# Hybrid Fourier and RG-LRU layer: the gate part of the adaLN product moved from GpSimd to narrow TensorE matmuls

## The chip, the cores and the metric

One core of a Trainium2 chip, one launch, all data in f32. The metric is the device time of a launch in microseconds, and of several launches the median.

## The reference

One layer of a diffusion backbone: a latent stream of 2048 positions by 1024 channels, with a context of 256 positions in front. A conditioning vector c gives shift, scale and gate through one product with w_ada (1024 by 3072). The modulated stream is projected into two branches with a gate path each: a 2-D Fourier transform (FNet) and a convolution with a bidirectional gated recurrence (RG-LRU, 4 heads). Both are gated, joined and projected out; the result is multiplied by `gate`, added to the stream and normalised.

```
def modulate(x, g, shift, scale):
    return rmsnorm(x, g) * (1.0 + scale) + shift
...
mod = jax.nn.silu(c) @ w_ada[l] + b_ada[l]
shift, scale, gate = jnp.split(mod[:, None, :], 3, axis=-1)
...
hx = modulate(x, norm_gain[l], shift, scale)
...
uf_x, gf_x, ul_x, gl_x = in_proj(hx, w_in[l])
...
r = jax.nn.sigmoid(block_diag(u, w_rg, b_rg).astype(jnp.float32))
i = jax.nn.sigmoid(block_diag(u, w_ig, b_ig).astype(jnp.float32))
log_a = -LRU_C * r * jax.nn.softplus(-lam.astype(jnp.float32))
a = jnp.exp(log_a)
bx = jnp.sqrt(-jnp.expm1(2.0 * log_a)) * (i * u.astype(jnp.float32))
...
y = jnp.concatenate([y_f * jax.nn.silu(g_f), y_l * jax.nn.silu(g_l)], axis=-1)
return y @ w_out
```

The change concerns only the columns of `mod` that become `gate` (the last 1024 of 3072), for the latent stream, and the order in which the second stage's work is written down.

## The kernel before

The program runs in stages on the one core. Stage 1 (list `S1`) does the modulation, the projections into the branches and the first transform; then comes the Fourier branch (list `STEPS`); stage 2 (list `S2`) does the projection into the gate path and the whole recurrence; stage 3 (list `S3`) does the output projection. Every list is a string of tokens. A token is one step of one helper, and PE, ACT and DVE take their instructions in exactly the order in which the tokens write them (manual_schedule, L718). The queues of SP and POOL are ordered by the framework's scheduler.

Nearly every product is done in three matmuls (mm3, L71 to L73): each f32 operand is split into a high part (cast on ACT) and a low part (subtraction on DVE).

The tokens of stage 2 that the text speaks of:

- `B0` to `B31` (p2_block): a block of the gate-path projection, 48 matmuls of 128x256 from `hg` and `wg` into a PSUM tile `pg`. `H` loads a piece of the modulated stream (L684), `Q` casts its high part on ACT (L689), `q` its low part on DVE (L694). `V` and `v` copy a finished `pg` out on ACT or DVE (L744), and a POOL queue stores it.
- `L`, `C`, `c` (L666 to L670, L785, L792): load a piece of a head, first tap of the convolution on ACT, three taps on DVE. `X` and `x` split the result `v` into `vh` (ACT, L798) and `vl` (DVE, L806) and the gate weights into their two parts (L802, L809).
- `g` (lru_gate): the recurrence's gate products from `vh`, `vl` and `gw`: `pl`, two stretches of 512 columns in a pool of its own (psl, 2 buffers), and for the first piece of a head also `pc`, 256 columns of context, in the pool ps2. Piece p has four of them, `gp.0` to `gp.3`. `S`, `T`, `E`, `R` on ACT and `s`, `I`, `N` on DVE (sigmoid, tanh, exp, root; products and scans) turn them into the recurrence.
- `G` (load_gate, L678): loads two of the eight pieces `gb` of w_ada's gate columns for one quarter q; two buffers. `A` (ada_gate) multiplies each piece with the silu of c (`sc_pad`) and sums it up, on GpSimd: L752 the product, L755 and L758 the sum of a piece's two halves, L759 the sum with `gsb`. `F` (ada_gate_fin) sums `gsb` over the partitions with a matmul of ones (L763, tile `go`) and adds it to `gate_bc` on DVE (L764). There are four quarters, and two `A` in each: 16 products and 28 sums.

The pool ps2 has four buffers of one bank, which `pg`, `pc` and `go` take in turn. In stage 1 the shift and scale columns of the same product are done by narrow matmuls on TensorE (ada_part, L131): 32 columns of `sc_pad` are the stationary operand, and four column groups of the array write four groups of 32 partitions of one PSUM tile.

The functions that the diff touches:

Of the kernel before, what the change touches and what calls it, by code (L numbers as in the profile page):

```python
# [9 lines left out]
F32 = mybir.dt.float32  # L10
# [42 lines left out]
def tile_layer(ctx, tc, xp, xnat, xt_in, ctxn, ctxt, w_ada, vec, bgate, fgain, w_in, w_g, w_four, w_gate, w_out,  # L53
               dct, d512, rmat, csts, out):
    nc = tc.nc
# [22 lines left out]
    sel, wsc = cst[:, 0:2], cst[:, 2:7]  # L78
    ones = const.tile([P, P], F32, name="ones")
# [9 lines left out]
    sc_pad = const.tile([P, KD, 32], F32, name="sc_pad")  # L89
# [24 lines left out]
    blks, raws, parts, pws = {}, {}, {}, {}  # L114
# [378 lines left out]
    p2 = p2s.enter_context(tc.tile_pool(name="p2", bufs=1, side="right", reuse_waits="tile"))  # L493
# [155 lines left out]
    X0 = CTX + GAP  # L649
# [75 lines left out]
    ps2 = pst.enter_context(tc.tile_pool(name="ps2", bufs=4, space=PSUM, reuse_waits="tile"))  # L725
# [21 lines left out]

    def ada_gate(q, h):
        for j in (2 * h, 2 * h + 1):
            blk = gbs.pop((q, j))  # L750
            cv = sc_pad[:, 2 * j:2 * j + 2, 0:1].to_broadcast([P, 2, 256])
            nc.gpsimd.tensor_tensor(out=blk, in0=blk, in1=cv, op=ALU.mult)  # L752
            if j == 0:
                acc = parts[q] = p2.tile([P, 256], F32, name=f"gsb{q}", tag="gsb", bufs=1)
                nc.gpsimd.tensor_tensor(out=acc, in0=blk[:, 0], in1=blk[:, 1], op=ALU.add)  # L755
            else:
                acc = parts[q]
                nc.gpsimd.tensor_tensor(out=blk[:, 0], in0=blk[:, 0], in1=blk[:, 1], op=ALU.add)  # L758
                nc.gpsimd.tensor_tensor(out=acc, in0=acc, in1=blk[:, 0], op=ALU.add)  # L759

    def ada_gate_fin(q):
        po = ps2.tile([P, 512], F32, name=f"go{q}", tag="pg")
        nc.tensor.matmul(po[:, 0:256], ones, parts.pop(q), start=True, stop=True)  # L763
        nc.vector.tensor_tensor(out=gate_bc[:, 256 * q:256 * q + 256], in0=gate_bc[:, 256 * q:256 * q + 256],  # L764
                                in1=po[:, 0:256], op=ALU.add)
# [92 lines left out]
    def lru_root(hd, pc):  # L858
        w, ts = WID[pc], st_[hd, pc][2]
        for d in range(2):  # L860
            nc.scalar.activation(out=ts[d][:, 0:w], in_=ts[d][:, 0:w], func=AF.Sqrt)
# [139 lines left out]
    def p3_lo(b, q, e):  # L1001
# [10 lines left out]
        "R": lambda p: lru_root(*pieces[p]), "I": lambda p, d: lru_input(*pieces[p], d), "N": lambda p, d: lru_scan(*pieces[p], d),  # L1012
        "A": ada_gate, "G": load_gate, "F": ada_gate_fin,
        "W": load_wo, "o": wo_gate, "O": wo_hi, "u": wo_tail,
        "Y": lambda i: (p3_first_load, p3_first_act, p3_first_prep)[i](ob[0]),
    }
    for x in S2:
        ops[x[0]](*(int(c) for c in x[1:].split(".")))
    xs, pos, s3 = {}, {}, {}
# [203 lines left out]
```

## Time and profile before

| | |
|---|---|
| Median of 3 runs | 677.46 us (676.71, 681.53, 677.46) |
| Span of the profiled execution, first to last instruction | 676.5 us |
| PE busy | 655.5 us, 97% of the span |
| DVE busy | 494.3 us, 73% |
| ACT busy | 403.2 us, 60% |
| POOL busy | 165.0 us, 24% |
| of which gate products and sums, L752, L755, L758, L759 | 23.1, 4.0, 15.7, 17.2 us |
| Stage 1 and Fourier branch | 0 to about 243 us |
| Stage 2 on PE | about 243 to 491.9 us |
| Stage 3 on PE | 492.0 to 676.5 us |

The profile is of one execution. The profiled execution has no device time of its own on record beside its span; the median of the three timed runs lies 1.0 us above that span. Busy shares are means over stages with different limits, so the rows further down are taken from the stage that the change touches. A PE matmul is pipelined: the step from one start to the next tells what it costs, and the duration in a row is longer. A plain f32 matmul shows as two instructions.

### The profile page before, as it was taken

To read this page: it belongs to the slowest core of one execution; us is meant where nothing else is said; L and a number is where in the kernel's file an instruction comes from. 1 tells how busy PE (TensorE), PEld (TensorE's weight loads), DVE (VectorE), ACT (ScalarE), POOL (GpSimd) and SP (SyncE) were. 2 spreads that over 40 slices of the span, in tenths; PEclk is the share of its full clock that TensorE was granted. 3 is DMA by queue.
4 is the path that set the end of the run, shared out by engine and by line. 5 is a ranking of instruction groups with operands and counts; after the bars stand their busy time and mean duration, and the time that the engine had idled before them with its cause. 6 is when DMAs were issued, how large, how long until landed. Compare 5 with 4: busy or idle time off the path is not lost.

```text
span 676.5 us, 10651 instructions
## 1 busy us (share of the span) xinstructions
PE 655.5 (97%) x4060; PEld 579.4 (86%) x4060; DVE 494.3 (73%) x767; ACT 403.2 (60%) x578; POOL 165.0 (24%) x214
## 2 busy tenths in 40 slices
PE   9999999999989989999996999999999999999996
PEld 8888888888978879899996999999988888888885
DVE  4767999877646697567999899997989455544523
ACT  5475777565624445577785877977753465543502
POOL 0000101031320276339756145131210000000000
PEclk8999999999988999999999899999999999999999
DMA  8996876548695884344443353432479566775211
GB/s 335 419 335 225 257 263 212 193 121 253 163 310 188 276 286 118 109 125 119 153 144 99 111 175 106 126 131 79 135 255 344 186 215 232 245 261 180 88 62 63
DMA packets 69898, 130.21 MB, mean 192 GB/s; under 512 B 7090, under 2 KB 39986, under 8 KB 69848
## 3 DMA queue, kind: packets, MB, share of 16 engines
q1 hardware_dynamic: 51080, 82.36, 37.0%
q0 software_dynamic: 12384, 39.00, 17.2%
q10 hardware_dynamic: 6384, 8.18, 3.7%
q8 instruction: 32, 0.52, 0.3%
q14 instruction: 18, 0.15, 0.1%
HBM read 91.24 MB, written 38.27 MB: 191 GB/s over the span
## 4 chain that ended last, share of the span: by engine, by line
PE 71%; DVE 13%; issue 5%; ACT 5%; DMA 4%; POOL 1%; DVEq 0%; SPq 0%; ACTq 0%; POOLq 0%
PE po L71 9%; PE po L72 9%; PE po L73 9%; PE pul L71 4%; PE pul L73 4%; PE pul L72 4%; PE pg L72 4%; PE pg L73 4%; PE pg L71 4%; DVE t L865 3%; PE ptt L71 2%; PE ptt L73 2%; PE ptt L72 2%; DVE v L792 2%; DVE t L872 1%
## 5 line engine op out<-in xcount | busy, mean ns | idle before, releaser
L71 PE MATMUL pg<-hg,wg 128*128 128x256 f32 x512 | 144.7, 283 | 1.9 <-DVE yf L646 1.9
L72 PE MATMUL pg<-hg,wg 128*128 128x256 f32 x512 | 144.3, 282 | 2.1 <-DVE hg L694 2.1
L73 PE MATMUL pg<-hg,wg 128*128 128x256 f32 x512 | 144.4, 282 | 0.3 <-DVE wg L545 0.3
L71 PE MATMUL po<-wo,y 128*128 128x512 f32 (+1 forms) x264 | 102.4, 388 | 0.0
L72 PE MATMUL po<-wo,y 128*128 128x512 f32 (+1 forms) x264 | 102.3, 387 | 0.0
L73 PE MATMUL po<-wo,y 128*128 128x512 f32 (+1 forms) x264 | 102.3, 387 | 0.0
L72 PEld LDWEIGHTS pg<-hg,wg 128*128 128x128 f32 x512 | 96.9, 189 | 3.5 <-DVE hg L694 2.5
L71 PEld LDWEIGHTS pg<-hg,wg 128*128 128x128 f32 x512 | 96.9, 189 | 3.3 <-ACT wg L544 2.3
L73 PEld LDWEIGHTS pg<-hg,wg 128*128 128x128 f32 x512 | 97.0, 189 | 0.5 <-DVE wg L545 0.5
L424 POOL DMA_DIRECT2D g_d<-gs x80 | 57.9, 725 | 96.7 <-DVE gs L744 53.0
L71 PEld LDWEIGHTS po<-wo,y 128*128 128x128 f32 x264 | 49.9, 189 | 11.0
L73 PEld LDWEIGHTS po<-wo,y 128*128 128x128 f32 x264 | 49.6, 188 | 11.2
L72 PEld LDWEIGHTS po<-wo,y 128*128 128x128 f32 x264 | 49.6, 188 | 10.7
L71 PE MATMUL pul<-hl,wu 128*128 128x512 f32 x124 | 49.9, 402 | 0.0
L1066 ACT ACTIVATE j<-xr 128x1024 bf16<-128x1024 f32 x15 | 15.9, 1058 | 55.5 <-DVE xr L1061 55.5
L73 PE MATMUL pul<-hl,wu 128*128 128x512 f32 x124 | 48.9, 395 | 0.0
L72 PE MATMUL pul<-hl,wu 128*128 128x512 f32 x124 | 48.8, 394 | 0.0
L1076 POOL DMA_DIRECT2D out_dram<-xr x15 | 8.0, 533 | 136.2 <-DVE xr L1075 136.2
L792 DVE SCALAR_TENSOR_TENSOR v<-up,vecs,v 128x1284 f32<-128x1284 f32 (+1 forms) x24 | 40.2, 1676 | 1.2 <-ACT v L785 0.6
L836 ACT ACTIVATE g<-pl,vecs 128x1024 f32<-128x1024 f32 x32 | 35.3, 1115 | 8.4 <-PE pl L73 8.4
L287 ACT ACTIVATE h<-xt,sh,gn 128x512 f32<-128x512 f32 x31 | 25.2, 813 | 19.4 <-DVE gn L149 10.4
L71 PE MATMUL ptt<-wf,eo 128*128 128x260 f32 (+1 forms) x128 | 36.5, 285 | 0.0
(298 smaller groups left out, 1569.8 us busy)
## 6 DMA issues: line engine op xcount, KB each, us to landing
xt<-in_xt_dram SPq DMA_DIRECT2D x16, 512.0 KB, 5.6
blk<-in_w_ada_dram SPq DMA_DIRECT2D x16, 512.0 KB, 8.1
hr<-h_d SPq DMA_DIRECT2D x32, 256.0 KB, 3.8
xr<-in_xnat_dram SPq DMA_DIRECT2D x16, 512.0 KB, 3.6
g<-g_d SPq DMA_DIRECT2D x15, 512.0 KB, 5.1
out_dram<-xr POOLq DMA_DIRECT2D x15, 512.0 KB, 2.9
dm<-in_dct_dram POOLq DMA_DIRECT2D x12, 514.0 KB, 6.7
x<-in_xp_dram SPq DMA_DIRECT2D x12, 512.0 KB, 5.6
```

The costliest lines, as they stand in the source:

```text
L71: nc.tensor.matmul(out_, lh, rh, start=first, stop=False, skip_group_check=skip)
L72: nc.tensor.matmul(out_, lh, rl, start=False, stop=False, skip_group_check=skip)
L73: nc.tensor.matmul(out_, ll, rh, start=False, stop=last, skip_group_check=skip)
L287: nc.scalar.activation(out=h[:, 0:n], in_=x, func=AF.Identity, scale=g, bias=b)
L424: queue.dma_start(dst[:, :, row:row + s1 - s0], s[:, :, P * i - off + s0:P * i - off + s1])
L792: nc.vector.scalar_tensor_tensor(out=v[:, 0:w], in0=up[:, j:j + w], scalar=cw[:, j:j + 1], in1=v[:, 0:w], op0=ALU.mult, op1=ALU.add)
L836: nc.scalar.activation(out=t[:, c0:c0 + cn], in_=pg[:, 0:cn], func=AF.Sigmoid, bias=vecs[:, q:q + 1])
L865: nc.vector.tensor_tensor_scan(sl(t), sl(a), sl(t), init, ALU.mult, ALU.add)
L872: nc.vector.tensor_tensor(out=t[:, 0:w], in0=t[:, 0:w], in1=iv[:, 0:w], op=ALU.mult)
L1066: nc.scalar.activation(out=junk, in_=xs[b][t], func=AF.Square, accum_out=s3[b, t][:, 0:1])
L1076: nc.gpsimd.dma_start(out[256 * b + P * t:256 * b + P * t + P], o)
```

## The change

The gate product of a quarter becomes eight narrow matmuls of `sc_pad` and `gb`, four in each `A`, into a PSUM tile `gpart` from the pool ps2; they are the same form as stage 1's. A new token `a` (ada_gate_copy) copies `gpart` to `gsb` on DVE, and the matmul in `F` takes a broadcast column of `sel` in place of ones. GpSimd does no arithmetic of it any more. The list `S2` is written in a new order; `S1`, `STEPS` and `S3` are as before.

```diff
@@ -39,7 +39,7 @@
-S2 = "H1.0 C0 c0 L1 X0 x0 Q1.0 H1.1 Q1.1 q1.1 q1.0 H1.2 B0 v0 ...
-    s0.2 A0.1 C2 X1 q1.3 x1 g0.3 S0.3 B7 Q2.1 Q2.0 c2 B4 T0 R0 ...
-    B8 H3.2 C3 Q3.0 V7 H3.3 g2.0 T1 s1.2 G2.0 q3.0 Q3.1 q3.1 c3 L4 E1 R1 v8 I1.1 S2.0 A1.1 N1.1 B9 ...
+S2 = "H1.1 H1.2 C0 H1.0 c0 Q1.1 X0 x0 Q1.0 H2.2 q1.1 q1.0 L1 B0 v0 ...
+    C2 X1 q1.3 g0.3 B7 A0.1 a0 Q2.0 Q2.1 S0.3 c2 x1 B4 T0 R0 ...
+    B8 A1.0 T1 G1.1 C3 Q3.0 V7 x2 H3.2 g2.0 s1.2 s1.1 R1 c3 q3.0 H4.1 Q3.1 q3.1 A1.1 E1 L4 v8 I1.0 I1.1 N1.1 B9 ...
 RB = 6
 SR = 72
 ZB = 7
@@ -746,21 +746,23 @@
         scatter(dst, gs, u, nc.gpsimd, (2 * hf, 2 * hf + 1), 256 * hf)
 
     def ada_gate(q, h):
+        if h == 0:
+            parts[q] = ps2.tile([P, 512], F32, name=f"gpart{q}", tag="pg")
         for j in (2 * h, 2 * h + 1):
             blk = gbs.pop((q, j))
-            cv = sc_pad[:, 2 * j:2 * j + 2, 0:1].to_broadcast([P, 2, 256])
-            nc.gpsimd.tensor_tensor(out=blk, in0=blk, in1=cv, op=ALU.mult)
-            if j == 0:
-                acc = parts[q] = p2.tile([P, 256], F32, name=f"gsb{q}", tag="gsb", bufs=1)
-                nc.gpsimd.tensor_tensor(out=acc, in0=blk[:, 0], in1=blk[:, 1], op=ALU.add)
-            else:
-                acc = parts[q]
-                nc.gpsimd.tensor_tensor(out=blk[:, 0], in0=blk[:, 0], in1=blk[:, 1], op=ALU.add)
-                nc.gpsimd.tensor_tensor(out=acc, in0=acc, in1=blk[:, 0], op=ALU.add)
+            for i in range(2):
+                g = (2 * j + i) % 4
+                nc.tensor.matmul(parts[q][32 * g:32 * g + 32, 0:256], sc_pad[:, 2 * j + i, :], blk[:, i, :],
+                                 start=h == 0, stop=h == 1, tile_position=(0, 32 * g))
+
+    def ada_gate_copy(q):
+        part = parts.pop(q)
+        parts[q] = p2.tile([P, 256], F32, name=f"gsb{q}", tag="gsb", bufs=1)
+        nc.vector.tensor_copy(parts[q], part[:, 0:256])
 
     def ada_gate_fin(q):
         po = ps2.tile([P, 512], F32, name=f"go{q}", tag="pg")
-        nc.tensor.matmul(po[:, 0:256], ones, parts.pop(q), start=True, stop=True)
+        nc.tensor.matmul(po[:, 0:256], sel[:, 0:1].to_broadcast([P, P]), parts.pop(q), start=True, stop=True)
         nc.vector.tensor_tensor(out=gate_bc[:, 256 * q:256 * q + 256], in0=gate_bc[:, 256 * q:256 * q + 256],
                                 in1=po[:, 0:256], op=ALU.add)
 
@@ -1010,7 +1012,7 @@
         "g": lambda p, i: lru_gate(*pieces[p], MS[i]), "S": lambda p, i: lru_sig(*pieces[p], MS[i]),
         "s": lambda p, i: lru_gated(*pieces[p], MS[i]), "T": lambda p: lru_tanh(*pieces[p]), "E": lambda p: lru_exp(*pieces[p]),
         "R": lambda p: lru_root(*pieces[p]), "I": lambda p, d: lru_input(*pieces[p], d), "N": lambda p, d: lru_scan(*pieces[p], d),
-        "A": ada_gate, "G": load_gate, "F": ada_gate_fin,
+        "A": ada_gate, "a": ada_gate_copy, "G": load_gate, "F": ada_gate_fin,
         "W": load_wo, "o": wo_gate, "O": wo_hi, "u": wo_tail,
         "Y": lambda i: (p3_first_load, p3_first_act, p3_first_prep)[i](ob[0]),
     }
```

Three places in the new order follow. Names carry the number of their tile, which differs between the two programs; lines from L764 on stand two lines further down in the changed kernel.

PE from the end of block `B8` (`pg_0_0`) to the start of `B9` (`pg_0_1`), before; `pc` and `pl` are the product `g2.0`:

```order
L73 MATMUL pg_0_0_3478<-hg_0_3_3420,wg_0_2759 128x256
L71 MATMUL pc_0_3543<-vh_0_3469,gw_3472 128x256
L72 MATMUL pc_0_3543<-vl_0_3470,gw_3472 128x256
L73 MATMUL pc_0_3543<-vh_0_3469,gw_3472 128x256
L71 MATMUL pl_0_0_260_3547<-vh_0_3469,gw_3472 128x512
L72 MATMUL pl_0_0_260_3547<-vl_0_3470,gw_3472 128x512
L73 MATMUL pl_0_0_260_3547<-vh_0_3469,gw_3472 128x512
L71 MATMUL pl_0_0_260_3547<-vh_0_3469,gw_3472 128x512
L72 MATMUL pl_0_0_260_3547<-vl_0_3470,gw_3472 128x512
L73 MATMUL pl_0_0_260_3547<-vh_0_3469,gw_3472 128x512
L71 MATMUL pg_0_1_3599<-hg_0_0_3219,wg_0_2379 128x256
```

The place from behind `B8` on now, where `gpart` is the narrow product of quarter 1 (each row of x2 is two matmuls):

```order
L755 MATMUL gpart_3515<-gb_0_3284,sc_pad 32x256 x2
L755 MATMUL gpart_3515<-gb_1_3286,sc_pad 32x256 x2
L71 MATMUL pc_0_3544<-vh_0_3459,gw_3462 128x256
L72 MATMUL pc_0_3544<-vl_0_3460,gw_3462 128x256
L73 MATMUL pc_0_3544<-vh_0_3459,gw_3462 128x256
L71 MATMUL pl_0_0_260_3548<-vh_0_3459,gw_3462 128x512
L72 MATMUL pl_0_0_260_3548<-vl_0_3460,gw_3462 128x512
L73 MATMUL pl_0_0_260_3548<-vh_0_3459,gw_3462 128x512
L71 MATMUL pl_0_0_260_3548<-vh_0_3459,gw_3462 128x512
L72 MATMUL pl_0_0_260_3548<-vl_0_3460,gw_3462 128x512
L73 MATMUL pl_0_0_260_3548<-vh_0_3459,gw_3462 128x512
L755 MATMUL gpart_3515<-gb_2_3524,sc_pad 32x256 x2
```

The two halves of quarter 1 now stand on PE around `g2.0`, nine matmuls apart (`A1.0` with `gb_0` and `gb_1`, then `A1.1`, which begins with `gb_2`); before, PE had nothing of them.

SP's queue at the loads of the second half of quarter 1 (`gb_2`, `gb_3`) and the first of quarter 2 (`gb_0`, `gb_1`), before:

```order
L684 DMA hr_1_3_3539<-h_d 128x2x256
L678 DMA gb_2_3429<-in_w_ada_dram 128x512
L659 DMA gwr_3570<-in_w_gate_dram 128x512
L678 DMA gb_3_3431<-in_w_ada_dram 128x512
L684 DMA hr_0_1_3650<-h_d 128x2x256
L684 DMA hr_0_0_3824<-h_d 128x2x256
L678 DMA gb_0_3559<-in_w_ada_dram 128x512
```

And now:

```order
L684 DMA hr_1_2_3540<-h_d 128x2x256
L659 DMA gwr_3574<-in_w_gate_dram 128x512
L678 DMA gb_2_3524<-in_w_ada_dram 128x512
L678 DMA gb_3_3526<-in_w_ada_dram 128x512
L678 DMA gb_0_3642<-in_w_ada_dram 128x512
L678 DMA gb_1_3644<-in_w_ada_dram 128x512
L666 DMA up_0_3576<-ul_d 128x256
```

The four loads stand in a row behind the load of the gate weights `gwr`. The two buffers of `gb` are still there, so a load waits for the reader of the piece before it: a POOL product before, a PE matmul now.

DVE at the split of the first head's second piece (`vl_1`, token `x1`), before; `v_0` are the taps `c2` of the next head, L840 is `s`:

```order
L840 TENSOR_TENSOR g_0_0_3036<-g_0_0_3036,v_0_2810 128x1284
L840 TENSOR_TENSOR g_0_0_3104<-g_0_0_3104,v_0_2810 128x1284
L694 TENSOR_TENSOR hg_1_3_2969<-hr_1_3_2890,hg_1_3_2969 128x512
L806 TENSOR_TENSOR vl_1_3149<-v_1_2894,vh_1_3148 128x1024
L819 MEMSET g_0_0_3153 128x4
L792 SCALAR_TENSOR_TENSOR v_0_3146<-up_0_2958,vecs,v_0_3146 128x1284 x3
L694 TENSOR_TENSOR hg_0_1_3217<-hr_0_1_3128,hg_0_1_3217 128x512
```

And now; `gsb` is the new copy `a0`:

```order
L842 TENSOR_TENSOR g_0_0_3106<-g_0_0_3106,v_0_2812 128x1284
L694 TENSOR_TENSOR hg_1_3_2967<-hr_1_3_2946,hg_1_3_2967 128x512
L821 MEMSET g_0_0_3141 128x4
L761 COPY gsb_3207<-gpart_3018 128x256
L794 SCALAR_TENSOR_TENSOR v_0_3135<-up_0_2956,vecs,v_0_3135 128x1284 x3
L808 TENSOR_TENSOR vl_1_3138<-v_1_2892,vh_1_3137 128x1024
L694 TENSOR_TENSOR hg_0_1_3211<-hr_0_1_3104,hg_0_1_3211 128x512
```

The split stands behind the copy and behind the three taps, where it stood ahead of the taps.

## Rows read from the trace of the kernel before

**Rows 1.** What PE waited for between 236 and 500 us: total, times, longest.

```profile
PE pc L72 <- DVE vl L806: 5.5, 1, 5.5
PE pg L72 <- DVE hg L694: 2.1, 2, 1.3
PE pg L71 <- DVE yf L646: 1.9, 1, 1.9
PE pc L71 <- ACT gs L744: 0.6, 1, 0.6
PE pl L72 <- DVE vl L806: 0.4, 1, 0.4
PE pg L73 <- DVE wg L545: 0.3, 1, 0.3
```

**Rows 2.** PE's timeline at the longest wait: start, duration, instruction, idle before it.

```profile
371.74 0.58 PE L72 MATMUL pc<-vl,gw 128*128 128x256 f32 x1 [5.46 <-DVE vl L806]
```

**Rows 3.** Busy time by stretch (columns named in the first line).

```profile
core 0: us, PE busy (x) PEld busy (x) DVE busy (x) ACT busy (x) POOL busy (x), PEclk, DMA share, GB/s
317.00:371.00 54.00, 48.45 (x367) 46.13 (x365) 53.20 (x44) 40.07 (x44) 37.08 (x34) 1.00 0.43 133
371.50:375.00 3.50, 3.24 (x8) 2.47 (x9) 3.46 (x5) 3.47 (x4) 0.53 (x1) 0.50 0.70 213
375.00:380.00 5.00, 5.00 (x33) 4.90 (x32) 2.58 (x7) 4.97 (x6) 1.44 (x2) 0.73 0.45 127
380.00:440.00 60.00, 60.00 (x454) 57.48 (x453) 57.60 (x54) 47.28 (x52) 21.54 (x24) 1.00 0.41 125
```

**Rows 4.** Groups on DVE between 317 and 371 us: count, busy us, mean ns.

```profile
L792 DVE SCALAR_TENSOR_TENSOR v<-up,vecs,v 128x1284 f32<-128x1284 f32 x3 | 6.2, 2056 | 0.1
...
L792 DVE SCALAR_TENSOR_TENSOR v<-up,vecs,v 128x1024 f32<-128x1024 f32 x3 | 5.0, 1680 | 0.1
L872 DVE TENSOR_TENSOR t<-t,g 128x1284 f32<-128x1284 f32 x2 | 4.1, 2071 | 0.1
...
L840 DVE TENSOR_TENSOR g<-g,v 128x1024 f32<-128x1024 f32 x2 | 3.3, 1640 | 0.0
```

**Rows 5.** Groups of two of these kinds on DVE from 456 us on.

```profile
L872 DVE TENSOR_TENSOR t<-t,g 128x1284 f32<-128x1284 f32 x2 | 3.0, 1496 | 0.1
...
L840 DVE TENSOR_TENSOR g<-g,v 128x1024 f32<-128x1024 f32 x2 | 2.4, 1208 | 0.0
```

**Rows 6.** DVE's timeline: single instructions, two of them beside an idle POOL.

```profile
282.94 1.55 DVE L792 SCALAR_TENSOR_TENSOR v<-up,vecs,v 128x1284 f32<-128x1284 f32 x1
...
370.20 1.48 DVE L806 TENSOR_TENSOR vl<-v,vh 128x1284 fp32r<-128x1284 f32 x1
...
372.81 1.28 DVE L792 SCALAR_TENSOR_TENSOR v<-up,vecs,v 128x1024 f32<-128x1024 f32 x1
```

**Rows 7.** DVE's timeline ahead of the first block of stage 2.

```profile
239.09 2.18 DVE L694 TENSOR_TENSOR hg<-hr,hg 128x512 fp32r<-128x512 f32 x2
241.19 2.55 DVE L545 TENSOR_TENSOR wg<-wgr,wg 128x512 fp32r<-128x512 f32 x2
...
250.88 0.68 DVE L545 TENSOR_TENSOR wg<-wgr,wg 128x512 fp32r<-128x512 f32 x1
```

**Rows 8.** PE's timeline in stage 1: narrow matmuls (L131) and what follows them.

```profile
47.48 1.07 PE L131 MATMUL part<-blk,sc_pad 128*32 128x256 f32 x16
48.48 0.50 PE L71 MATMUL pul<-hl,wu 128*128 128x512 f32 x1
48.81 0.39 PE L72 MATMUL pul<-hl,wu 128*128 128x512 f32 x1
49.04 0.39 PE L73 MATMUL pul<-hl,wu 128*128 128x512 f32 x1
```

**Rows 9.** Tile `gb`: from its load's issue to landing, us, min/median/max.

```profile
DMA to landing us min/median/max: 2.4/3.0/7.3
```

**Rows 10.** Line L137, the copy of stage 1's narrow product: duration ns min/median/max.

```profile
L137 DVE COPY psb<-part x8: 414/424/427, 13.3 to 62.5; 128x256 f32<-128x256 f32 x8
```

More of the change, by code (lines that the diff above doesn't have):

```diff
@@ new lines @@
+S2 = "H1.1 H1.2 C0 H1.0 c0 Q1.1 X0 x0 Q1.0 H2.2 q1.1 q1.0 L1 B0 v0 C1 c1 B1 H1.3 G0.1 Q1.2 L2 V1 Q1.3 B2 A0.0 g0.0 g0.1 S0.1 B3 H2.0 S0.0 q1.2 H2.1 g0.2 V3 s0.1 v2 S0.2 s0.2 C2 X1 q1.3 g0.3 B7 A0.1 a0 Q2.0 Q2.1 S0.3 c2 x1 B4 T0 R0 q2.1 v4 F0 G1.0 E0 B5 L3 I0.1 Q2.2 H2.3 q2.2 g1.0 g1.1 S1.0 q2.0 B6 v5 Q2.3 q2.3 N0.1 S1.1 H3.1 I0.0 g1.3 N0.0 H3.3 H3.0 g1.2 V6 X2 S1.2 S1.3 B8 A1.0 T1 G1.1 C3 Q3.0 V7 x2 H3.2 g2.0 s1.2 s1.1 R1 c3 q3.0 H4.1 Q3.1 q3.1 A1.1 E1 L4 v8 I1.0 I1.1 N1.1 B9 G2.0 g2.1 S2.1 S2.0 a1 B10 s2.1 g2.2 Q3.2 Q3.3 S2.2 V10 V9 q3.2 s2.2 H4.0 B11 F1 Q4.1 V11 C4 g2.3 X3 q3.3 x3 S2.3 Q4.0 c4 L5 H4.2 T2 H4.3 N1.0 E2 q4.1 R2 q4.0 B12 A2.0 v12 g3.0 B13 G2.1 I2.1 N2.1 I2.0 g3.1 S3.1 Q4.2 S3.0 s3.1 B14 q4.2 Q4.3 g3.2 N2.0 V14 S3.2 g3.3 s3.2 X4 H5.1 v13 x4 S3.3 q4.3 C5 c5 L6 T3 H5.0 A2.1 G3.0 H5.2 E3 B15 H5.3 a2 g4.0 R3 S4.0 v15 I3.1 Q5.0 B16 F2 N3.1 B17 Q5.2 Q5.1 q5.0 V16 g4.1 Q5.3 S4.1 g4.2 g4.3 q5.2 S4.2 s4.2 V17 A3.0 B18 S4.3 B19 C6 I3.0 H6.3 s4.1 X5 q5.1 H6.0 N3.0 q5.3 G3.1 v18 x5 c6 L7 v19 T4 R4 H6.1 E4 g5.0 I4.1 S5.0 Q6.0 g5.1 A3.1 I4.0 N4.1 S5.1 a3 s5.1 B20 Q6.1 H6.2 V20 N4.0 B21 F3 g5.2 v21 g5.3 Q6.2 S5.2 s5.2 Q6.3 q6.2 X6 x6 q6.0 q6.1 S5.3 C7 B22 c7 T5 R5 q6.3 E5 v22 I5.0 g6.0 B23 g6.1 S6.0 I5.1 B24 N5.1 g6.2 v24 V23 H7.0 N5.0 S6.1 S6.2 H7.1 g6.3 s6.1 s6.2 Q7.0 H7.2 X7 Q7.2 Q7.1 B25 H7.3 x7 S6.3 q7.0 q7.2 q7.1 T6 Q7.3 R6 W0 g7.0 v25 W3 q7.3 E6 S7.0 W1 B26 I6.1 o1 N6.1 g7.1 S7.1 s7.1 B27 V26 V27 Y0 Y1 o0 W2 W4 g7.2 Y2 O1 o2 W6 W7 O2 O0 o3 u2 W5 I6.0 u1 S7.2 o4 O3 g7.3 s7.2 S7.3 T7 u0 W10 W9 E7 O4 u3 N6.0 o5 o6 O6 O5 o7 u6 B28 u5 B29 W8 v29 O7 B30 v28 B31 u4 W11 u7 R7 V30 V31".split()
```

1 line of the change is left out of this document (removed).

## Prediction

> **What bounds the kernel now.** I read the busy shares first: PE works 97% of the span, so the time is PE's own work plus the few places where PE stands still. Next come PE's waits, to find those places. All that count lie in stage 2 [rows 1]: one wait of 5.5 us for `vl`, two for `hg` (2.1 together), 1.9 for `yf`, and three small ones, 10.8 us in all (5.5 + 2.1 + 1.9 + 0.6 + 0.4 + 0.3). Except for the 0.6, which waits for ACT to empty a bank, they wait for DVE. The long one is the first product with `vl` of piece 4 (token `g4.0`) at 371.74 [rows 2].
>
> Then the stretches [rows 3]. Before that wait DVE is busy 53.2 of 54 us: it is the engine that is late. After it the granted clock of PE is 0.50 until 375 and 0.73 until 380, then 1.00 again. That is the lower of its levels (1.2 of 2.4 GHz), after PE had stood still for 5.46 us. From 371.74 to 375 at half speed loses 1.6 us and 5 us at 0.73 lose 1.35: about 3 us more for the same stall.
>
> Last, why DVE is late. In the same stretch POOL is busy 37.1 us [rows 3], and DVE's instructions take longer than elsewhere: the taps 2056 and 1680 ns against 1.55 and 1.28 us, L872 2071 against 1496, L840 1640 against 1208 [rows 4 to 6]. Those four groups alone are 1.5 + 1.2 + 1.15 + 0.86 = 4.7 us over their usual durations. They are 10 of the 44 instructions; I estimate the whole stretch at 7.7 us by working the other groups in the same way.
>
> **GpSimd's arithmetic goes.** 16 products and 28 sums, 60 us on POOL by the table. POOL is not the bound, so this gives nothing by itself. What it gives is DVE's delay back. At the first block of stage 2 four instructions of two kinds take 2.18 and 2.55 us for two, where one alone of the second kind takes 0.68 [rows 7]: 2.55 - 1.36 = 1.2 us on one pair, and there are two pairs of each kind ahead of the second block, some 4 us. So the waits for `yf` (1.9) and `wg` (0.3) should go.
>
> The Trainium skill, "SBUF — State Buffer", section "Terms", says that GpSimd and DVE take one pair of ports under an exclusive lock and that the loser blocks for the whole instruction. By that rule taken alone, DVE could lose most of POOL's 37 us in the stretch; the rows show a fifth of that, so the sum goes by the rows.
>
> **The long wait.** DVE ends `vl` at 370.20 + 1.48 = 371.7 [rows 6]. Without the stretch it is 364.0 to 367.0 (less 7.7 or 4.7), plus two new copies `a0` and `a1` ahead of it, at 0.42 each by stage 1's copy [rows 10]: 364.8 to 367.8. PE came to the place at 371.74 - 5.46 = 366.3. Now it comes earlier by the waits ahead of it (1.9 + 0.3 + 0.6 + 2.1 = 4.9) and later by six narrow sets (3.6, below) and one new wait (1.5, below): 366.5. So the wait is between nothing and 1.3 us where it was 5.5, and without a long stall the slow clock (3.0) goes too. Taking the slack end as the nearer, I leave 0.5 here.
>
> **The narrow matmuls.** 32 matmuls on PE, in eight sets of four, two instructions each. Stage 1 has the same form: 16 instructions take 48.48 - 47.48 = 1.00 us from start to start, and the matmul behind them steps 0.33 where the next steps 0.23 [rows 8]. A set of eight is 0.50 + 0.10 = 0.60, and eight sets 4.8 us, all on the path, since PE is the bound. If a set also loses 0.1 on entry it is 5.6; if the last step hides, 4.0. The matmul in `F` has the same shape as before, so 0.
>
> The Trainium skill, "TensorEngine Tiling (Array Packing)", section "Tiling Modes", says that a change of the tiling mode drains TensorE. This speaks against the change: 16 switches instead of none. The row shows such a drain as 0.10 us or less on leaving; by the rule at its worst (rival (d)) the gain would be 2.6 us instead of 6.4.
>
> **A new wait at quarter 1.** `A1.0` and `A1.1` stand nine matmuls apart, 3 x 0.12 + 6 x 0.23 = 1.76 us (the step of 512 columns is 0.23 [rows 8]; 256 columns at half). The pieces of `A1.1` go into the two buffers that `A1.0` reads, so their loads start only when `A1.0` has run, and a load takes 2.4 to 7.3 us, 3.0 in the median [rows 9]. Issued 0.3 and 0.6 us after `A1.0`'s start at best, the second lands about 3.6 to 4 us after it; PE is there after 0.6 + 1.76 = 2.4. So 1.2 to 1.6 us; I take 1.5, bounds 0.5 and 5.5. Queued behind it on PE are `B9` and all that follows; on SP the loads for quarter 2 and `up`, which are needed much later. The other quarters' halves are two blocks or more apart, so their loads are hidden.
>
> **A bank and the copies.** `gpart` holds one of the four banks of ps2 from the first half to the copy, so `pg` and `pc` have three. The only bank wait now is 0.6 us [rows 1]. In the four spans some 20 tiles ask for a bank, and by the order on the engines each former reader stands well ahead; between 0 and 1 us each, I take the 0.6 that is there to be repeated once or so. Four copies on DVE, 4 x 0.42 = 1.7 us, lie off PE's path once DVE has its time back.
>
> **The new order.** The split `x1` on DVE now stands behind the copy `a0` and the taps `c2` (0.4 + 4.7 us at 1.55 a tap [rows 6]). `a0` itself waits for PE's `A0.1`, which comes right behind block `B7`; queued behind it are those taps and `x1`. `g1.0`, which needs it, stands behind `B4` and `B5`, over 11 us of PE, so this is hidden; if not, it costs 1 us at the most. The two waits for `hg` fall with the stretch. Moving `F` and the loads gives nothing. For small waits that remain or appear (the 0.6 for a bank, or one for a split of a later piece) I set 0.6, bounds 0 and 3.
>
> **Sum.** Off: 10.8 + 3.0 = 13.8. On: 4.8 + 1.5 + 0.5 + 0.6 = 7.4. The gain is 6.4 us, so the span of 676.5 becomes 670.1. Stage 3 moves along with PE: its inputs come from the same DVE chain, and PE has no wait there. The median of the runs lies 1.0 above the span; 671.0.
>
> **Rivals.**
> (a) Everything fits: no wait at `g4.0`, none small, and the load of `A1.1` lands in 2.4. For it: 10.8 us of waits with few causes, and DVE gets back more than the rows shown. Against: the nine matmuls cover too little of a load. 13.8 - 4.8 - 0.5 = 8.5 off: 668.9.
> (b) The change doesn't do what it says: POOL goes quiet, but `vl` of piece 4 stays late, since DVE is 98% full in that stretch and other work fills what comes free (ACT's exponentials and roots set when DVE's inputs are there). The stall and the slow clock stay, 5.5 + 3.0, less the 0.5 already counted: 671.0 + 8.0 = 679.0. Against: the stretched rows [rows 4] lie directly ahead of the `vl`.
> (c) Slower: the bank. If `gpart` makes PE wait at each of the 20 requests, at 1 us each (the wait of 0.6 that is there is of this kind), that is 20 us on top: 691. It makes the kernel slower by over 1% from 13.2 us on, 0.65 us a request. Against: in the order most former readers are a block (5.6 us) ahead.
> (d) The narrow sets cost more: PE runs empty at each of the 16 changes of form, a whole matmul's passage each (0.58 at half the clock [rows 2], so 0.29), 4.6 us in place of 8 x 0.10. With the rest as forecast, 671.0 + 3.8 = 674.8. Against: the 0.10 of [rows 8].
>
> **How the numbers follow.** The forecast 0.42, (a) 0.24, (b) 0.17, (c) 0.08, (d) 0.09. A measurement of this kernel can tell about 1%, 6.8 us, from no change, so the bound for faster is 670.7 and for slower 684.2. The forecast lies almost on the bound: half of it and somewhat more than all of (a)'s middle fall under it, 0.21 + 0.23 = 0.44 and a little for the DVE share not shown, 0.46. Slower is (c) and a little for a load of 7.3 us that brings a stall like today's, 0.10. Same: 0.44. The range takes in (a) with a margin of 4 for the small terms at their good ends, and (b) with one: 665.0 to 680.5.
>
> **What would show it.** Right: no wait over 1 us for `vl` on PE, and the clock at 1.00 from 243 us on; a wait of 1 to 2 us at the second `gpart` set after `B8`, for a load; eight sets of about 0.6; the taps on DVE near 1.55 us; POOL without arithmetic. Wrong: waits of PE for banks at `pg` or `pc` in the span of a `gpart`, a `vl` wait at the first product of piece 4 that is still several us, or narrow sets well over 1 us.

## The result and the profile after

The changed kernel takes 671.26 us (median of 11 runs) against 677.94 us (11 runs): ratio 0.9907, interval 0.9884 to 0.9930, so a gain of 4.7 to 7.9 us. A second set of runs, with the same kernel unedited (below), gave 671.49 against 676.81: 0.9924, 0.9896 to 0.9952. The forecast was 671.0.

PE's waits of the changed kernel from 220 to 500 us, which answer to [rows 1]; lines from L764 on have moved by two:

```profile
PE pl L72 <- DVE vl L808: 1.2, 1, 1.2
PE gpart L755 <- DMA gb<-in_w_ada_dram: 1.1, 2, 1.0
PE pg L71 <- ACT bs L636: 0.7, 1, 0.7
```

Of the 10.8 us of waits in [rows 1] five kinds, 10.4 us, are gone. The sixth, 0.4 us for `vl`, stood at the first product of piece 7 (`g7.0`) and still does; it is 1.2 now. With it 3.0 us of waits stand there: the others are 1.15 for the new load, as forecast, and 0.7 for ACT at the first block, where 1.9 for `yf` stood. Its stretches, which answer to [rows 3]:

```profile
317.00:371.00 54.00, 53.99 (x412) 50.36 (x411) 44.90 (x46) 40.53 (x44) 11.21 (x16) 1.00 0.48 143
371.00:380.00 9.00, 9.00 (x76) 8.91 (x75) 6.76 (x12) 8.94 (x10) 1.45 (x2) 1.00 0.47 156
380.00:440.00 60.00, 60.00 (x456) 56.01 (x455) 55.06 (x53) 44.59 (x50) 11.22 (x16) 1.00 0.38 119
```

PE (second column) is full, the granted clock (third from the right) stays at 1.00 where it had been 0.50 and 0.73, and DVE (fourth) is busy 44.9 of 54 us in place of 53.2. POOL (sixth) keeps 11.2 us, all of it issues of DMAs; its arithmetic is gone. DVE's groups in that first stretch, beside [rows 4]:

```profile
L794 DVE SCALAR_TENSOR_TENSOR v<-up,vecs,v 128x1284 f32<-128x1284 f32 x3 | 4.7, 1555 | 0.1
L874 DVE TENSOR_TENSOR t<-t,g 128x1284 f32<-128x1284 f32 x2 | 3.0, 1496 | 0.1
...
L842 DVE TENSOR_TENSOR g<-g,v 128x1024 f32<-128x1024 f32 x2 | 2.4, 1218 | 0.0
...
L794 DVE SCALAR_TENSOR_TENSOR v<-up,vecs,v 128x1024 f32<-128x1024 f32 x1 | 1.3, 1287 | 0.0
```

Each of these groups has the duration that [rows 5, 6] show away from POOL's arithmetic: 1555 for 2056 ns, 1287 for 1680, 1496 for 2071, 1218 for 1640.

PE's timeline at one narrow set, at quarter 1's second half, and at the product that waited 5.46 us before [rows 2]:

```profile
281.78 0.28 PE L73 MATMUL pg<-hg,wg 128*128 128x256 f32 x1
281.99 0.64 PE L755 MATMUL gpart<-gb,sc_pad 128*32 128x256 f32 x8
282.56 0.39 PE L71 MATMUL pg<-hg,wg 128*128 128x256 f32 x1
282.79 0.28 PE L72 MATMUL pg<-hg,wg 128*128 128x256 f32 x1
...
315.05 0.63 PE L755 MATMUL gpart<-gb,sc_pad 128*32 128x256 f32 x4 [0.99 <-DMA gb<-in_w_ada_dram]
315.84 0.63 PE L755 MATMUL gpart<-gb,sc_pad 128*32 128x256 f32 x4 [0.16 <-DMA gb<-in_w_ada_dram]
...
368.96 0.28 PE L71 MATMUL pc<-vh,gw 128*128 128x256 f32 x1
369.08 0.28 PE L72 MATMUL pc<-vl,gw 128*128 128x256 f32 x1
369.38 0.39 PE L73 MATMUL pc<-vh,gw 128*128 128x256 f32 x1
```

From the start of the last `pg` to that of the second one behind the set are 1.01 us, where two steps of 0.12 would do without it: a set costs 0.77 us (0.09 on entry, 0.57 for its own steps, 0.11 on leaving). The wait for the load is 0.99 + 0.16. At the third place the step from L71 to L72 is 0.12, so there is no wait for `vl`. DVE's timeline there:

```profile
367.23 1.49 DVE L808 TENSOR_TENSOR vl<-v,vh 128x1284 fp32r<-128x1284 f32 x1
368.63 0.69 DVE L811 TENSOR_TENSOR gw<-gwr,gw 128x512 fp32r<-128x512 f32 x1
```

DVE ends `vl` at 368.72, 0.36 us before PE starts the matmul that reads it. It ends the low part of `gw`, which L73 reads, at 369.32, and the step from L72 to L73 is 0.30 where 0.12 is usual, so 0.18 us is all that is left of the long wait.

One plain caution on the profiled execution: its span is 673.5 us, 4.4 above the middle one of the 11 runs (669.1), and it began stage 2 later than the profile of before did. So the experiments are compared by stage 2 on PE's timeline, from the first `pg` (less the wait ahead of it) to the first `po`. Before: 243.18 to 492.04, 248.9 us. After: 245.06 to 488.96, 243.9 us, 4.95 less. Stage 3 is 184.5 in both. A second profile of the changed kernel has 244.4, so differences of half a microsecond are not read.

### The profile page after: what moved, and what is told of

Same layout as the page of the kernel before. It is cut to its first block, busy times and chain, and to the rows that moved or that the text cites. A ratio compares the mean times of both kernels' runs of the same rounds, so it can differ in the third digit from the quotient of the medians.

```text
span 673.5 us, 10726 instructions
## 1 busy us (share of the span) xinstructions
PE 659.3 (98%) x4124; PEld 578.8 (86%) x4124; DVE 477.2 (71%) x771; ACT 402.9 (60%) x578; POOL 105.4 (16%) x170
## 4 chain that ended last, share of the span: by engine, by line
PE 92%; DMA 3%; ACT 2%; DVE 1%; issue 1%; SPq 0%; DVEq 0%; ACTq 0%
PE po L71 9%; PE pg L71 9%; PE po L72 9%; PE po L73 9%; PE pg L73 9%; PE pg L72 9%; PE pul L71 5%; PE pul L73 4%; PE pul L72 4%; PE ptt L71 2%; PE ptt L73 2%; PE ptt L72 2%; PE pl L72 2%; PE pl L73 2%; PE pl L71 2%; DMA w4a<-in_w_four_dram 1%
## 5 line engine op out<-in xcount | busy, mean ns | idle before, releaser
L71 PE MATMUL pg<-hg,wg 128*128 128x256 f32 x512 | 144.2, 282 | 0.7 <-ACT bs L636 0.7
L73 PE MATMUL pg<-hg,wg 128*128 128x256 f32 x512 | 143.8, 281 | 0.0
L72 PE MATMUL pg<-hg,wg 128*128 128x256 f32 x512 | 143.5, 280 | 0.0
L71 PE MATMUL po<-wo,y 128*128 128x512 f32 (+1 forms) x264 | 102.4, 388 | 0.0
L72 PE MATMUL po<-wo,y 128*128 128x512 f32 (+1 forms) x264 | 102.3, 387 | 0.0
L73 PE MATMUL po<-wo,y 128*128 128x512 f32 (+1 forms) x264 | 102.3, 387 | 0.0
L71 PEld LDWEIGHTS pg<-hg,wg 128*128 128x128 f32 x512 | 96.3, 188 | 4.0 <-ACT wg L544 1.1
L72 PEld LDWEIGHTS pg<-hg,wg 128*128 128x128 f32 x512 | 96.3, 188 | 0.7
L73 PEld LDWEIGHTS pg<-hg,wg 128*128 128x128 f32 x512 | 96.4, 188 | 0.0
L71 PEld LDWEIGHTS po<-wo,y 128*128 128x128 f32 x264 | 49.9, 189 | 11.0
L73 PEld LDWEIGHTS po<-wo,y 128*128 128x128 f32 x264 | 49.6, 188 | 11.2
L72 PEld LDWEIGHTS po<-wo,y 128*128 128x128 f32 x264 | 49.6, 188 | 10.7
L71 PE MATMUL pul<-hl,wu 128*128 128x512 f32 x124 | 49.9, 402 | 0.0
L73 PE MATMUL pul<-hl,wu 128*128 128x512 f32 x124 | 49.0, 395 | 0.0
L72 PE MATMUL pul<-hl,wu 128*128 128x512 f32 x124 | 48.8, 394 | 0.0
L287 ACT ACTIVATE h<-xt,sh,gn 128x512 f32<-128x512 f32 x31 | 25.2, 813 | 19.8 <-DVE gn L149 10.4
L71 PE MATMUL ptt<-wf,eo 128*128 128x260 f32 (+1 forms) x128 | 36.5, 286 | 0.0
L73 PE MATMUL ptt<-wf,eo 128*128 128x260 f32 (+1 forms) x128 | 36.3, 283 | 0.0
L72 PE MATMUL ptt<-wf,eo 128*128 128x260 f32 (+1 forms) x128 | 36.2, 283 | 0.0
```

The costliest lines, as they stand in the source:

```text
L71: nc.tensor.matmul(out_, lh, rh, start=first, stop=False, skip_group_check=skip)
L72: nc.tensor.matmul(out_, lh, rl, start=False, stop=False, skip_group_check=skip)
L73: nc.tensor.matmul(out_, ll, rh, start=False, stop=last, skip_group_check=skip)
L287: nc.scalar.activation(out=h[:, 0:n], in_=x, func=AF.Identity, scale=g, bias=b)
```

## The experiments

Theory 1: the gain is DVE's, freed of GpSimd's arithmetic; the price is eight sets on PE. The rival: the new order makes the gain. The table gives the medians and stage 2 of each profile, worked out as above; the text takes them one by one.

| kernel | median us | before beside it | stage 2, us |
|---|---|---|---|
| before | 677.94 | | 248.9 |
| changed | 671.26 | 677.94 | 243.9 |
| changed, again | 671.49 | 676.81 | 244.4 |
| matmuls, old order | 676.89 | 677.15 | 247.5 |
| GpSimd, new order | 683.85 | 677.15 | 254.9 |
| no gate product | 679.79 | 677.15 | 250.4 |
| GpSimd quiet, old order | 664.88 | 677.15 | 235.8 |
| GpSimd quiet, new order | 667.29 | 677.78 | 237.6 |
| matmuls, old order, A1 close | 675.95 | 677.78 | 247.8 |
| sets twice | 675.40 | 677.78 | 246.6 |
| two edits | 669.20 | 677.78 | 242.1 |
| three edits | 668.72 | 676.81 | 240.6 |
| last quarter on GpSimd | 676.12 | 676.81 | 249.7 |

**GpSimd quiet in the old order.** The kernel before with

```diff
-            nc.gpsimd.tensor_tensor(out=blk, in0=blk, in1=cv, op=ALU.mult)
...
-                nc.gpsimd.tensor_tensor(out=acc, in0=blk[:, 0], in1=blk[:, 1], op=ALU.add)
+                nc.gpsimd.memset(acc, 0.0)
+                nc.gpsimd.tensor_tensor(out=acc[:, 0:1], in0=blk[:, 0, 0:1], in1=blk[:, 1, 0:1], op=ALU.add)
...
-                nc.gpsimd.tensor_tensor(out=blk[:, 0], in0=blk[:, 0], in1=blk[:, 1], op=ALU.add)
-                nc.gpsimd.tensor_tensor(out=acc, in0=acc, in1=blk[:, 0], op=ALU.add)
+                nc.gpsimd.tensor_tensor(out=acc[:, 0:1], in0=blk[:, 0, 0:1], in1=blk[:, 1, 0:1], op=ALU.add)
```

> The kernel before with GpSimd's arithmetic cut to one column of each piece (and one fill of gsb per quarter), so the gate is not computed; order and loads stay. Theory 1: DVE's taps take 1.55 and 1.28 us throughout, the long wait and the slow clock behind it go, and so do the waits at the start of stage 2: 11 to 14 us off, 664 to 667. Rival (DVE's order and ACT set the long wait): 3 us off at most, 675 to 678.

664.88 us, ratio 0.9810 (0.9777 to 0.9844). PE's waits from 236 to 500 us are

```profile
PE pl L72 <- DVE vl L804: 1.2, 1, 1.2
PE pc L73 <- DVE gw L807: 0.2, 1, 0.2
```

and DVE's taps in stage 2 (12 of each form, 236 to 456 us)

```profile
L790 DVE SCALAR_TENSOR_TENSOR v<-up,vecs,v 128x1284 f32<-128x1284 f32 x12 | 18.6, 1553 | 0.3
L790 DVE SCALAR_TENSOR_TENSOR v<-up,vecs,v 128x1024 f32<-128x1024 f32 x12 | 15.4, 1282 | 0.3
```

Nothing but GpSimd's arithmetic was taken away, and with it went the long wait, the slow clock (the granted clock is 1.00 all through stage 2) and the waits at the stage's start: stage 2 is 13.1 us shorter, of the 13.8 that the forecast put on these. This settles what those waits came from. The 1.2 us that are left stand at `g7.0`, as in the changed kernel. Here it is the old order, without sets and with GpSimd quiet, so none of the three makes that wait.

**The order alone.** The changed kernel with the GpSimd code of before, `a` empty.

> The new order with the product left on GpSimd as before. Theory 1: DVE's instructions are as slow as before in the stretch, and PE keeps several us of waits for DVE in stage 2, the long one at piece 4 among them, without the narrow sets; 674 to 679. Rival (the order makes the gain): stage 2 has under 2 us of waits and no narrow sets; 663 to 666.

683.85 us, slower than before: 1.0085 (1.0045 to 1.0124). Its waits on PE, 236 to 500 us:

```profile
PE pc L72 <- DVE vl L809: 5.6, 1, 5.6
PE pl L72 <- DVE vl L809: 3.1, 2, 1.9
PE pg L71 <- DVE gs L744: 2.9, 1, 2.9
PE pg L73 <- DVE wg L545: 2.0, 1, 2.0
PE pg L71 <- DVE yf L646: 1.7, 1, 1.7
```

The long wait is back whole, and more waits for DVE with it, beyond the range of either theory: a slow DVE costs more in the new order than in the old one. Why was not followed up. The order doesn't make the gain.

**The matmuls alone.** The changed kernel with the list of before; the copies are put in, and `F3` goes a block back.

```diff
-... A0.1 C2 X1 q1.3 x1 g0.3 S0.3 B7 Q2.1 Q2.0 c2 B4 ...
+... A0.1 C2 X1 q1.3 x1 g0.3 S0.3 B7 Q2.1 Q2.0 c2 a0 B4 ...
```

> The narrow matmuls in the order of before: the tokens stand as before, only the copies are put in about a block behind their second half (a0 ahead of B4, a1 ahead of B10, a2 ahead of B16, a3 behind B22 with F3 behind B23). Theory 1 (the gain is DVE's, freed of GpSimd's arithmetic): PE's 5.5 us wait for vl of piece 4 is gone here too, the eight sets cost about 6 us; 671 to 674. Rival (the new order makes the gain): the long wait stays and the sets come on top; 679 to 684.

676.89 us, 0.9990 (0.9966 to 1.0013): no gain, above the 671 to 674 of theory 1. The long wait is gone, but there is a new one, in the row of the waits

```profile
PE pg L71 <- ACT g L838: 3.6, 1, 3.6
```

at 321.62, block `B10`: a block waits for a bank that ACT's sigmoid of `g2.0` still reads, until 321.56. The quiet kernel has the same order on PE and ACT but no `gpart`, and no such wait, though ACT is as late there:

```profile
318.11 0.47 ACT L834 ACTIVATE g<-pc,vecs 128x256 f32<-128x256 f32 x1
```

Its `B10` began at 313.73, 4.4 us ahead of that sigmoid. So here the bank of rival (c) is real. A variant with quarter 1 held shorter (`A1.0` behind `B8`, `A1.1` behind `B9`, `a1` ahead of `B11`):

> The narrow matmuls in the order of before, but quarter 1's first half moved behind B8 and its second behind B9, with the copy ahead of B11, so that its bank is held for one block where it was held for four products. Theory (the 3.6 us wait for a bank at B10 is there because gpart holds the fourth bank): that wait goes and no other comes, 672 to 674. Rival (ACT's sigmoids are late whatever gpart holds): the wait stays or moves to another bank request, 676 to 678.

675.95 us, 0.9982 (0.9948 to 1.0016); the wait is 3.5 us and stays. This misses, and tells nothing against the bank: `gpart` was still held at `B10`, and it was hardly held shorter. DVE came to the copy only at 334.92, 27.7 us after the first set, where it had been 30.5.

A token's place in the list is not its time. In the changed kernel `a1` stands ahead of `B10`, but the copy runs at 330.84, and `B10` begins at 323.92, so there too `gpart` holds its bank. There is no wait, since PE asks later: `g2.1` stands ahead of `B10`, and ACT's first sigmoid behind it has read its tile by 323.21, 0.7 us before. The run with two edits, further down, shows `B10` waiting for just that sigmoid. With the matmuls the new order is worth some 3 us of stage 2 (247.5 against 243.9 and 244.4). A variant of the old order without `gpart` held at `B10` was not tried.

**The price of the sets.** First try: the narrow matmuls left out.

```diff
         for j in (2 * h, 2 * h + 1):
-            blk = gbs.pop((q, j))
...
+            gbs.pop((q, j))
...
-        nc.vector.tensor_copy(parts[q], part[:, 0:256])
+        nc.vector.memset(parts[q], 0.0)
```

> The changed kernel with the narrow matmuls of the gate left out: the loads stay, gsb is filled with zeros on DVE in place of the copy, so the gate is its bias alone. Theory 1: eight sets at 0.77 us from start to start over what stands there without them (6.1) and the load's wait of 1.2 are on PE's path; about 7 us under the changed kernel, 663 to 665. Rival (the sets hide mostly in the passage of the matmuls around them, and banks cost more): under 3 us off, 668 to 671; or over 10 off if banks held by gpart cost as well, 661 or less.

679.79 us, slower than the kernel with the matmuls. The run can't be used for the price, and its timeline of SP's queue says why:

```profile
246.42 17.63 SPq L678 DMA_DIRECT2D gb<-in_w_ada_dram  x10
264.22 0.33 SPq L670 DMA_DIRECT2D up<-ul_d  x1
```

Loads that nobody reads are ordered early: ten stand in a row ahead of `up`, ACT has the convolution's first tap late, and PE waits 8.4 us for a bank behind it. The second try keeps a reader: the quiet GpSimd code in the new order.

> The new order with the product back on GpSimd, cut to one column of each piece as in the other quiet kernel (the gate is not computed), so that every load still waits for a reader. Theory 1: no sets on PE and no slow DVE: 6 to 7.5 us under the changed kernel, 663.5 to 666, much like the quiet kernel in the old order (664.9). Rival (the new order is worth or costs something by itself, beside GpSimd): more than 2 us away from 664.9.

667.29 us, 0.9834 (0.9783 to 0.9885); the median is above theory 1's range and 2.4 from the old order's, as the rival had it. The medians are of four runs each and their ratios' intervals overlap, but stage 2 tells the same: 237.6, against 235.8 in the old order, so the new order costs 1.8 us where no `gpart` is. All of that stands at piece 4: PE waits 2.05 us there for `vl` and `gw`, 0.2 in the old order. Against it the changed kernel's 243.9 and 244.4 are 6.3 and 6.8 more. Eight sets at 0.77 make 6.2. The wait for the load (1.15 and 1.3) and the one at the stage's start (0.7 and 1.3) come on top, and the wait at piece 4 shrinks by 1.9: 6.15 and 6.9 in all. Last, every set doubled:

```diff
+            for n in range(2):
...
-                                 start=h == 0, stop=h == 1, tile_position=(0, 32 * g))
+                                     start=h == 0 and n == 0, stop=h == 1 and n == 1, tile_position=(0, 32 * g))
```

> The changed kernel with each pair of narrow matmuls issued twice into the same sum (the gate's product comes out doubled). Theory (a set costs its own length on PE, 0.57, and the changes of form 0.1 at each end): 8 x 0.57 = 4.6 us on top of 671.3, 675 to 677. Rival (most of the price is the change of form, not the matmuls): 1 to 2 us on top, 672 to 673.5.

675.40 us, 0.9953 (0.9921 to 0.9985), at the low end of the theory's range. A set tells a smaller number than 0.57:

```profile
260.25 1.08 PE L756 MATMUL gpart<-gb,sc_pad 128*32 128x256 f32 x16
261.26 0.39 PE L71 MATMUL pc<-vh,gw 128*128 128x256 f32 x1
```

16 instructions take 1.01 us from start to start, 8 take 0.57. So the matmuls of a set cost 0.44, and 0.77 - 0.44 = 0.33 us do not grow with the set. I take these for the change of form into the set and out of it; no run takes them apart further. Stage 2 agrees: it is 2.7 and 2.2 us over the changed kernel's two profiles while its waits are 0.9 and 1.6 shorter, which makes 0.45 and 0.48 for each doubled set. The theory was nearer than the rival, and both had a part of it.

**A better version.** Three edits to the list of the changed kernel, tried as two and then three. First `A1.1` behind `B9`, and `x7` ahead of `s6.1 s6.2`:

> The changed kernel with A1.1 moved behind B9 (its copy ahead of B11) and the split x7 moved ahead of the two products s6.1 and s6.2 on DVE. Theory: the load's wait (1.15) and the wait for vl at g7.0 (1.2) go, nothing takes their place: 668.5 to 669.5. Rival (bank wait or a late s6 takes their place): 670.5 to 672.5.

669.20 us, 0.9870 (0.9828 to 0.9911), stage 2 at 242.1. Both waits went; 0.5 for a bank at `B10` and two for `hg`, 0.7, came. PE came to `B10` earlier by the load's wait, and the sigmoid ended at 318.69, 0.06 before `B10` began. Then

```diff
-... B8 A1.0 T1 ... g2.0 ... A1.1 ... B9 G2.0 g2.1 S2.1 S2.0 a1 B10 ... B11 F1 ... x3 S2.3 ... B12 A2.0 ...
+... B8 T1 ... g2.0 ... B9 g2.1 S2.1 S2.0 B10 A1.0 ... B11 A1.1 G2.0 ... x3 a1 S2.3 ... B12 F1 A2.0 ...
-... g6.3 s6.1 s6.2 Q7.0 H7.2 X7 ... x7 S6.3 q7.0 q7.2 q7.1 T6 ...
+... g6.3 Q7.0 H7.2 X7 ... x7 S6.3 q7.0 q7.2 q7.1 s6.1 s6.2 T6 ...
```

> The changed kernel with quarter 1's sets moved behind B10 and B11 (copy behind x3, F1 behind B12), x7 moved up and s6.1 and s6.2 put behind the low parts q7. Theory: in the run with two edits three small waits were left in stage 2 (0.55 for a bank, 0.49 and 0.24 for hg); with gpart out of the span in which ACT is late with g2.0 and the low parts ahead of s6 they go, stage 2 takes 240.5 to 241.2 on PE's timeline, the time 667.5 to 668.8. Rival (DVE or a bank elsewhere takes their place): stage 2 at 242 or more, 669.5 to 671.

668.72 us, 0.9874 (0.9838 to 0.9910), and one wait left in stage 2:

```profile
PE pg L72 <- DVE hg L694: 0.8, 1, 0.8
```

Here `gpart` takes its bank behind `B10`, which begins at 315.36 without a wait, 1.75 us ahead of the same sigmoid (317.11): the bank shows a second time. Stage 2 is 240.6: 3.3 to 3.8 under the changed kernel. By medians side by side it is 2.8 under it (668.72 and 671.49). The quiet kernel in the old order plus eight sets would be 235.8 + 6.2 = 242.0, so with these edits the new order costs nothing against the old one any more. Of the 1.4 between the two, 0.6 are shorter waits (0.8 in place of 1.4). The changed kernel beside it:

> The changed kernel once more, unedited. In its first profile stage 2 was 4.9 us shorter than before on PE's timeline, while the medians differ by 6.7. Theory (the stage is all that the change moves, and the rest of the difference is the spread of what runs before stage 2): stage 2 at 243.9 again within 0.5, and a difference of medians in this call of 4 to 7 us. Rival (stage 2's length itself varies, or the first stages gain too): stage 2 more than 0.5 away from 243.9.

Stage 2 is 244.4, and the medians differ by 5.3. Stage 2 comes out alike twice, as the theory had it. It is 4.95 and 4.47 us shorter than before, and both lie inside the intervals of the medians (4.7 to 7.9 and 3.2 to 7.0); that the rest of the 6.7 us is spread of the runs is likely and not shown.

**A quarter back on GpSimd**, in the kernel with two edits (`ada_gate` and `ada_gate_fin` of before where q is 3).

> The kernel with two edits (A1.1 later, x7 earlier), with the last quarter's product back on GpSimd as before. Theory (DVE is late by whatever GpSimd takes): the sets of that quarter go from PE (1.5 off) but DVE, 55 of 60 us busy there, loses some 4 us and PE gets waits for vl of pieces 5 to 7, of 1 to 4 us: stage 2 at 242 to 245, 669 to 672. Rival (late in stage 2 DVE has slack enough): no new wait, stage 2 at 240.5, 667.5.

676.12 us, 0.9988 (0.9956 to 1.0020): as slow as the kernel before, and stage 2 is well over the 242 to 245 of the theory. Of the waits on PE from 236 to 500 us the two largest are

```profile
PE pl L72 <- DVE vl L835: 2.9, 1, 2.9
PE pc L73 <- DVE gw L838: 2.4, 1, 2.4
```

The second shows the slowing in a single instruction of DVE, beside POOL's first two products:

```profile
365.77 3.13 DVE L838 TENSOR_TENSOR gw<-gwr,gw 128x512 fp32r<-128x512 f32 x1
366.29 2.05 POOL L762 TENSOR_TENSOR gb<-gb,sc_pad 128x512 f32<-128x512 f32 x2
```

With the product on PE the same instruction takes 0.68 us. One quarter on GpSimd takes back 7.6 us of stage 2 (242.1 to 249.7) to save 1.5 on PE: 5.3 are these two waits, and behind the longer one the granted clock is 0.50 and 0.80 for 10 us. A wait of 0.8 at the stage's start is none of it, since GpSimd begins on the quarter at 366. At pieces 4 and 5 DVE has no slack either.

## Why the prediction was right

The time and the sign were right, and the mechanism. That the median came within 0.3 us of 671.0 is luck: the terms erred by 2 us, and the medians differ by more than stage 2 does. Of the signs that the prediction named, the load's wait, the clock, the taps and POOL came as written; a wait over 1 us for `vl` stood at piece 7, and the sets cost 0.77. It put 0.46 on a gain over 1% and 0.44 on a change within 1%; the gain was 0.93%, so the likelier of the two, by a hair, did not come. Term by term:

- The waits that go: 13.8 us with the slow clock. All went but the 0.4 at piece 7; taking GpSimd's work alone away made stage 2 13.1 shorter. By the durations of the changed kernel, group by group, DVE had lost 8.5 us in the stretch, where 7.7 was the estimate. POOL's 37 us there were not all arithmetic, as the text took them: some 26 were, the rest issues of DMAs that stay. So DVE lost about a third of the arithmetic's time and not a fifth.
- The long wait at piece 4: between nothing and 1.3, 0.5 taken. It was 0.18. The margin is thin, 0.36 us at `vl`. Stage 2 began 1.9 us later in this execution than before; less that, `vl` ended at 366.8 and PE came at 367.2, where 364.8 to 367.8 and 366.5 stood in the text.
- The narrow sets: 0.60 each, 4.8 in all. This is the term that was mis-sized: 0.77 each, 6.2 in all. Halving stage 1's 1.00 us for 16 instructions [rows 8] put the fixed part of a set at nothing; a set of eight takes 0.57, and entry costs 0.09, which I had kept only as a bound. The Trainium skill, "TensorEngine Tiling (Array Packing)", section "Tiling Modes", has a change of mode drain the engine. The doubled sets agree that there is a price beside the matmuls, 0.33 us a set, between the 0.10 of the sum and the 0.58 of rival (d).
- The wait at quarter 1: 1.5 taken; 1.15, and 1.3 in the second profile.
- Small waits and the bank: 0.6 taken. No wait for a bank, but 1.2 for `vl` at piece 7 (with the 0.4 that was there before) and 0.7 for ACT at the stage's start, 1.9 in all.

So the sum comes to 13.8 off and 6.2 + 1.15 + 0.2 + 1.9 = 9.4 on, a gain of 4.4; stage 2 shows 4.95 and 4.47. The forecast's 6.4 was 1.5 to 2 us too good, and lies inside both intervals of the medians, which can't tell the two apart.

Of the rivals, (a) fails by 1.15 and 1.9 us of waits and the dearer sets; two and three edits show that most of it was to be had. (b) falls with the quiet kernel: what made DVE late at piece 4 was GpSimd, and nothing else of that size. (c) did not come about in the changed kernel; its mechanism is shown in the old order, as one wait of 3.6 us where ACT is late with a tile, and not as a little at each request. (d) is half right: 0.33 of its 0.58 a set.

## What to carry to other kernels

Work on an engine that is not the bound can still set the time by slowing its neighbour: compare an instruction's duration beside it with the same instruction elsewhere, and cut that work to one column to see the whole of its price (13 us of stage 2 here, for 60 us on POOL). When such work goes to the engine that is the bound, its own length is the floor of the price, so take it in few long sets, hold its PSUM bank across no place where a reader is late, check in the trace when the copy that frees it really runs, and start its loads early (two blocks ahead were enough here, nine matmuls were not). An experiment that leaves a reader out also moves the loads; keep a small reader.

## What the runs showed that was not expected

The time at which stage 2 begins varied by 4.5 us between profiles of kernels with the same first two stages: 240.59 in the run with three edits, 245.06 in the changed kernel. In the latter's first 20 us a wait of PE at the start was 1.3 us against 0.3 before, and the granted clock was 0.61 and 0.50 in the slices from 10 to 15 and 15 to 20 us, against 0.75 and 0.57 before. For a change worth 5 us, a stage of the trace is the better measure than a single span.

An order that is good for one engine's load is bad for another: with GpSimd's arithmetic the new order lost 6.1 us of stage 2 (248.86 to 254.95), with the matmuls it gained some 3.
